# A written TensorE order for the scan stage of a hybrid S5 / attention layer

## The chip, the core and the metric

The kernel runs on one core of one Trainium2 chip. The metric is device time in microseconds: the median of three executions. TensorE (PE, with its weight loads shown apart as PEld), VectorE (DVE), ScalarE (ACT) and GpSimd (POOL) each run their own instruction stream in order; SyncE (SP) issues nearly all the transfers.

## What is computed

One layer of a trunk, on 128 context tokens and 128 latent tokens that share all weights (256 columns in every product), in float32:

```python
mod = silu(cond) @ w_mod + b_mod        # shift1, scale1, gate1, shift2, scale2, gate2
xm  = rmsnorm(x) * (1 + scale1) + shift1
u, q, k, v, gate_ssm, gate_attn = split(xm @ w_in)
S   = s5(u)          # 64 groups x 16 channels, 64 complex states, scanned both ways
S   = (gelu(S) * sigmoid(gelu(S) @ w_glu)) @ w_ssm_o
A   = windowed_attention(q, k, v, sink) @ w_attn_o
x  += gate1 * ((sigmoid(gate_ssm) * S + sigmoid(gate_attn) * A) @ w_out)
x  += gate2 * conv_ffn(rmsnorm(x) * (1 + scale2) + shift2)
```

For each direction of the S5 branch `bu = b_bar @ u`, `h[t] = lam_bar * h[t-1] + bu[t]` and `y += real(c @ h)`; the last states are outputs too.

## The kernel before

Nearly all the work is products with streamed weights. Each weight tile of 512 KB (`[128, 2, 512]` float32) is fetched once into one of five buffers named `raw` (RAW = 5), rounded on ACT to a high part (`hi`, L184), and the remainder is taken on DVE (`lo`, L185); there are three pairs of `hi` and `lo` (HL = 3). Three matmuls then stand for one float32 product (L395, L396, L397). One such tile makes 24 matmuls; it is called an F unit below. The raw buffer is free when `lo` is done.

The modulation `w_mod` is multiplied unsplit: two raw tiles make one burst of matmuls (L263), called M below, and both buffers are held until TensorE has done it. When sixteen such bursts are done, `mod_pp` (L268, L272, L276) moves their sums into place.

`drive()` walks a list of steps. A step is an F unit, half of an M, or a piece of other work. It issues the loads in the list's order as buffers come free, and emits `hi` and `lo` of the next units ahead of the step that uses them, at a raised priority. The list's order is not the order of execution: everything is emitted inside a `TileContext` whose scheduler reorders each engine's instructions by a timeline that it works out itself.

The attention and the S5 branch's set-up are woven into F units of `w_in`. Then comes the scan stage, the subject here. It goes over eight quarters `q` of the state. In each, `bu_mm` multiplies by `BL` (L1375), `rot_in` turns the result (L1388 to L1391), `scans` runs two scans (L1397), `rot_out` turns back into `H` (L1405 to L1407, finals L1409), and `yout` multiplies by `CL` and a small matrix `MI` (L1416, L1425), with a Gelu on ACT (L1428). What the next quarters need is made beside it: `m_gen` makes `MI` (TensorE L1338, ACT L1349 and `dg`, DVE L1344 to L1346); `b_prod` and `b_exp` make `BL`: two products on DVE, an expansion on ACT into `BD` (L1300) and `B` (L1302), and, for each of two directions, two groups of four transposes (L1308) into the only buffer of the PSUM tag `misc`, each copied to `BL` by ACT (L1309); `c_prod` and `c_exp` make `CL` (L1328, L1329); `tables` and `decay` make `tab` and `R`.

Beside the scans TensorE has 56 F units (8 of the attention gate's projection, 16 of `w_attn_o`, 32 of the scan gate's projection with sigmoids on ACT, L672) and 48 bursts M in three groups of sixteen. `weave` deals these evenly into the list of scan steps (`weave(ssm.stages(), (fill, FF0, FF1), (modfill, MF0, MF1))`); the scheduler then decides where each stands. The tail of the attention, which stands ahead of this stage in the list, consists of scores (L625), softmax (DVE L626 to L643, ACT L638), transposes of the weights (L651, copied by L652), products (L658, copied by L663, L664) and four transposes of rows for the convolution (L585).

## Time and profile before

| | |
|---|---|
| median of three executions | 1551.19 us (1549.31 to 1555.21) |
| the profiled execution | 1552.15 us |
| its span, first to last instruction | 1550.1 us |
| TensorE busy | 1491.0 us, 96% |
| weight loads busy | 1311.1 us, 85% |
| VectorE, ScalarE busy | 1007.7 us, 65%; 766.7 us, 49% |
| granted clock of TensorE, mean | 0.99 of 2.4 GHz |
| DMA | 349.18 MB, mean 225 GB/s |

A line of the view by stretches gives a stretch's length, then for each engine (TensorE, its weight loads, VectorE, ScalarE, GpSimd) its busy time and the number of instructions, then the granted clock, the DMA engines' busy share and the rate. A timeline line gives the start, the duration, the engine, the line of the kernel, the operation, the tile written and the tiles read. Matmuls are pipelined, so the distance between starts tells more than the duration of one. Traced matmul counts of L263, L1375 and L1425 are two for each instruction.

### The profile page before, as it was taken

To read this page: it belongs to the slowest core of one execution; us is meant where nothing else is said; L and a number is where in the kernel's file an instruction comes from. 1 tells how busy PE (TensorE), PEld (TensorE's weight loads), DVE (VectorE), ACT (ScalarE), POOL (GpSimd) and SP (SyncE) were. 2 spreads that over 40 slices of the span, in tenths; PEclk is the share of its full clock that TensorE was granted. 3 is DMA by queue.
4 is the path that set the end of the run, shared out by engine and by line. 5 is a ranking of instruction groups with operands and counts; after the bars stand their busy time and mean duration, and the time that the engine had idled before them with its cause. 6 is when DMAs were issued, how large, how long until landed. Compare 5 with 4: busy or idle time off the path is not lost.

```text
span 1550.1 us, 29294 instructions
## 1 busy us (share of the span) xinstructions
PE 1491.0 (96%) x11871; PEld 1311.1 (85%) x11871; DVE 1007.7 (65%) x1541; ACT 766.7 (49%) x1191; POOL 85.7 (6%) x179
## 2 busy tenths in 40 slices
PE   6989999999899999999999999999999999999997
PEld 5758799778677788998689999889999988999986
DVE  4997776468866566765665656655665655666665
ACT  6335537645545666544554544433544543545543
POOL 2000004022321000000000000000000000000000
PEclk9999999999999999999999999999999999999999
DMA  9999754774676677975566676765555565566563
GB/s 352 352 340 321 286 196 157 258 277 156 209 241 238 240 250 274 310 244 192 172 242 235 205 245 201 238 200 190 176 192 181 181 197 191 175 205 197 170 203 123
DMA packets 104246, 349.18 MB, mean 225 GB/s; under 512 B 13900, under 2 KB 16628, under 8 KB 104112
## 3 DMA queue, kind: packets, MB, share of 16 engines
q1 hardware_dynamic: 98576, 344.20, 64.9%
q0 software_dynamic: 5312, 3.05, 0.8%
q8 instruction: 93, 1.52, 0.4%
q14 instruction: 41, 0.34, 0.1%
q10 hardware_dynamic: 224, 0.08, 0.0%
HBM read 343.76 MB, written 2.46 MB: 223 GB/s over the span
## 4 chain that ended last, share of the span: by engine, by line
PE 83%; DMA 8%; DVE 4%; ACT 2%; issue 1%; POOL 1%; SPq 0%; DVEq 0%; ACTq 0%
PE acc L395 16%; PE acc L396 16%; PE acc L397 16%; PE acc L421 8%; PE acc L422 8%; PE acc L423 8%; PE mod L263 5%; DMA raw<-in_w_mod_dram 2%; DMA raw<-in_w_in_dram 2%; PE bu L1375 1%; DVE lo L185 1%; DMA rw<-in_w_mod_dram 1%; DMA U<-u 1%; DMA raw<-in_w_attn_o_dram 1%; ACT hi L184 1%
## 5 line engine op out<-in xcount | busy, mean ns | idle before, releaser
L185 DVE TENSOR_TENSOR lo<-raw,hi 128x1024 fp32r<-128x1024 f32 (+1 forms) x456 | 538.7, 1186 | 444.8 <-ACT hi L184 442.8
L184 ACT ACTIVATE hi<-raw 128x1024 fp32r<-128x1024 f32 (+1 forms) x456 | 468.5, 1029 | 609.1 <-PE acc L397 260.7
L395 PE MATMUL acc<-yh,lo 128*128 128x256 f32 x1408 | 400.0, 284 | 0.0
L396 PE MATMUL acc<-yl,hi 128*128 128x256 f32 x1408 | 398.8, 283 | 0.0
L397 PE MATMUL acc<-yh,hi 128*128 128x256 f32 x1408 | 398.7, 283 | 0.0
L395 PEld LDWEIGHTS acc<-yh,lo 128*128 128x128 f32 x1408 | 270.3, 192 | 8.9 <-DVE lo L185 4.2
L396 PEld LDWEIGHTS acc<-yl,hi 128*128 128x128 f32 x1408 | 270.3, 192 | 0.1
L397 PEld LDWEIGHTS acc<-yh,hi 128*128 128x128 f32 x1408 | 270.2, 192 | 0.0
L395 PE MATMUL acc<-xh,lo 128*128 128x256 f32 x568 | 166.8, 294 | 9.3 <-ACT sig L672 4.8
L396 PE MATMUL acc<-xl,hi 128*128 128x256 f32 x568 | 163.4, 288 | 0.0
L397 PE MATMUL acc<-xh,hi 128*128 128x256 f32 x568 | 163.1, 287 | 0.0
L422 PE MATMUL acc<-lo,ff 128*128 128x512 f32 x352 | 136.8, 389 | 0.0
L423 PE MATMUL acc<-hi,ff 128*128 128x512 f32 x352 | 136.8, 389 | 0.0
L395 PEld LDWEIGHTS acc<-xh,lo 128*128 128x128 f32 x568 | 109.2, 192 | 31.4 <-DVE lo L185 6.9
L421 PE MATMUL acc<-hi,ff 128*128 128x512 f32 x352 | 127.8, 390 | 0.0
L396 PEld LDWEIGHTS acc<-xl,hi 128*128 128x128 f32 x568 | 109.6, 193 | 2.4 <-issue 2.2
L397 PEld LDWEIGHTS acc<-xh,hi 128*128 128x128 f32 x568 | 109.5, 193 | 0.7 <-issue 0.7
L263 PE MATMUL mod<-raw,cst 128*32 128x512 f32 x480 | 72.2, 631 | 8.0 <-DMA raw<-in_w_mod_dram 7.2
L421 PEld LDWEIGHTS acc<-hi,ff 128*128 128x128 f32 x352 | 66.1, 188 | 14.7 <-issue 1.1
L423 PEld LDWEIGHTS acc<-hi,ff 128*128 128x128 f32 x352 | 66.1, 188 | 13.7
L422 PEld LDWEIGHTS acc<-lo,ff 128*128 128x128 f32 x352 | 66.1, 188 | 13.5
L1316 POOL DMA_DIRECT2D U<-u x128 | 62.6, 497 | 159.6 <-PE bu L1375 138.5
(365 smaller groups left out, 2149.3 us busy)
## 6 DMA issues: line engine op xcount, KB each, us to landing
raw<-in_w_up_dram SPq DMA_DIRECT2D x176, 512.0 KB, 4.2
raw<-in_w_mod_dram SPq DMA_DIRECT2D x120, 512.0 KB, 5.1
raw<-in_w_in_dram SPq DMA_DIRECT2D x88, 512.0 KB, 4.5
raw<-in_w_down_dram SPq DMA_DIRECT2D x88, 512.0 KB, 4.3
rw<-in_w_mod_dram SPq DMA_DIRECT2D x56, 512.0 KB, 6.6
raw<-in_w_out_dram SPq DMA_DIRECT2D x32, 512.0 KB, 4.1
rw<-in_w_mod_first_dram SPq DMA_DIRECT2D x16, 512.0 KB, 7.4
raw<-in_w_in_dram SPq DMA_DIRECT2D x32, 256.0 KB, 6.1
```

The costliest lines, as they stand in the source:

```text
L184: ACT(th[:, w], raws[n][:, w], AF.Copy)
L185: TT(tl[:, w], raws[n][:, w], f32(th[:, w]), OP.subtract)
L263: return MM(acc[32 * j:32 * j + 32], cst[:, kt, 6 - 2 * b:38 - 2 * b], rhs, start=start, stop=stop, skip_group_check=True, tile_position=( ...
L395: MM(o, wl, xh, start=start, stop=False, skip_group_check=True)
L396: MM(o, wh, xl, start=False, stop=False, skip_group_check=True)
L397: MM(o, wh, xh, start=False, stop=stop, skip_group_check=True)
L421: MM(accs[s], xl, hi[:, j, :], start=(kt == first), stop=False)
L422: MM(accs[s], xh, lo[:, j, :], start=False, stop=False)
L423: lastmm[0] = MM(accs[s], xh, hi[:, j, :], start=False, stop=(kt == last - 1))
L1316: nc.gpsimd.dma_start(G["U4", qd][32 * e:32 * e + 32, q, :], u[32 * q:32 * q + 32, 64 * e:64 * e + 64])
L1375: MM(bu[:, ri, x], BL[d][:, ri, q, :], u[:, :, ::-1] if d else u, start=(x == 0), stop=True, skip_group_check=True)
```

## The change

Only the scan stage and the pieces that it is made of are changed.

- A region `tc.manual_schedule(engines={PE})` opens ahead of the stage's first step and closes behind its last. Inside it TensorE's instructions run in the order of the program; the other engines are still ordered by the scheduler.
- `weave` is no longer used here. `stages()` now writes one period for each quarter, with the marks `"fill"` (F) and `"mod"` (M) at fixed places: seven F and six M in each. The marks are replaced by the 56 F units and the 48 bursts in their old order.
- A period on TensorE is: `bu_mm`, M, F, M, `m_gen`, F, M, F, transposes, M, transposes, F, F, transposes, M, transposes, F, `yout`, F, M.
- `b_exp` is split: `b_bd` is the expansion on ACT, `b_tr` one group of four transposes with its copy to `BL`. `b_prod` of the next quarter but one stands ahead of `yout`.
- `finals()` stands behind the region.

In the changed file the same code stands some twenty lines lower: `bu_mm` is L1396, the transposes L1329, their copies L1330, the expansion L1318, `MI` L1370, `yout` L1437 and L1446.

```diff
-    weave(ssm.stages(), (fill, FF0, FF1), (modfill, MF0, MF1))
+    plan = ssm.stages()
+    region = ExitStack()
+    step(lambda: region.enter_context(tc.manual_schedule(engines={mybir.EngineType.PE})))
+    left = {"fill": [[u] for u in fill], "mod": []}
...
+    share = {k: (len(v), plan.count(k)) for k, v in left.items()}
...
+    step(region.close)
+    steps.append(ssm.finals())
...
+    def b_tr(qd, d, ri):
+        if (d, ri) == (0, 0):
+            G["BL"] = []
+        if ri == 0:
+            G["BL"].append(S4([128, 2, 4, 128], "BL"))
+        p = PS([128, 4, 128], "misc")
+        for q in range(4):
+            TR(p[:, q, :], G["BD"][:, ri, q].rearrange("p e g c -> p (e g c)"), ident)
+        ACT(G["BL"][d][:, ri], p, AF.Copy)
...
     def stages():
-        st = [s(u_exp, 0), s(u_exp, 1), s(c_exp, 0), s(bu_mm, 0), s(rot_in, 0, 0), s(m_gen, 0), s(rot_in, 0, 1)] + b_side(1) + c_side(1)
+        F, M = "fill", "mod"
+        st = [s(u_exp, 0), s(u_exp, 1), s(c_exp, 0)] + b_side(1)
         for q in range(8):
-            st += [s(scans, q), s(rot_out, q, 0), s(rot_out, q, 1)]
-            if q < 7:
-                st += [s(decay, q + 1), s(bu_mm, q + 1)]
-            if q < 6:
-                st += [s(u_exp, q + 2)]
-            st += [s(yout, q)]
...
-        st.append(Step(finals))
+            n = q + 1
+            more = n < 8
+            st += [s(bu_mm, q), s(rot_in, q, 0), M, s(rot_in, q, 1), F, s(scans, q)]
+            st += [s(decay, n)] if more else []
+            st += [M, s(m_gen, q), F, s(rot_out, q, 0), M]
+            st += [s(b_bd, n, 0)] if more else []
+            st += [s(rot_out, q, 1), F]
+            st += [s(tables, n), s(b_tr, n, 0, 0), M, s(b_tr, n, 0, 1), F] if more else [M, F]
+            st += ([s(b_bd, n, 1)] if more else []) + c_side(n) + [F]
+            st += [s(b_tr, n, 1, 0), M, s(b_tr, n, 1, 1), F] if more else [M, F]
+            st += b_side(n + 1) + [s(yout, q)]
+            st += [s(c_exp, n)] if more else []
+            st += [s(u_exp, q + 2)] if q < 6 else []
+            st += [F, M]
```

Where the instructions stand now is shown at three places; in the rows `x4` is the number of like instructions in a row.

**TensorE at the end of the attention's tail.** `misc<-kc,P` are the transposes of the softmax weights, `misc<-P,..` the products, `misc<-kc,BD` the first transposes of the scan stage, `acc` an F unit and `mod` a burst. Before, around the first row of `bu`:

```order
L396 MATMUL acc<-xl,hi 128x256
L397 MATMUL acc<-xh,hi 128x256
L263 MATMUL mod<-raw,cst 32x512 x4
L1308 MATMUL misc<-kc,BD 128x128 x4
L1375 MATMUL bu<-U_3341,BL 128x64
L395 MATMUL acc<-oh,lo 128x256
L396 MATMUL acc<-ol,hi 128x256
L397 MATMUL acc<-oh,hi 128x256
```

After, up to the first burst:

```order
L658 MATMUL misc<-P,pg 128x512
L651 MATMUL misc<-kc,P 128x128 x8
L658 MATMUL misc<-P,pg 128x512
L658 MATMUL misc<-P,kT 128x512
L1329 MATMUL misc<-kc,BD 128x128 x8
L1396 MATMUL bu<-U_3337,BL 128x64
L585 MATMUL misc<-kc,rows 128x128 x2
L1329 MATMUL misc<-kc,BD 128x128 x8
L1396 MATMUL bu<-U_3337,BL 128x64 x8
L585 MATMUL misc<-kc,rows 128x128
L1396 MATMUL bu<-U_3337,BL 128x64 x7
L263 MATMUL mod<-raw,cst 32x512 x4
```

Before, an M and F units stand between the transposes and behind the first row of `bu`; now the tail's steps and the first `bu` stand in one piece, with the first M behind them.

**ScalarE in the middle of a quarter.** `hi` is the high part of the next F unit, `MI` belongs to `m_gen`, `BL` is the copy out of the transposes' PSUM buffer, `BD` the expansion. Before:

```order
L1309 ACTIVATE BL<-misc 128x512
L1300 ACTIVATE BD<-tB 64x16x16 x2
L184 ACTIVATE hi<-raw 128x1024
L1349 ACTIVATE MI<-y 32x7x32 x4
L1342 ACTIVATE dg<-kc,vecA 128x32
L184 ACTIVATE hi<-raw 128x1024
L1309 ACTIVATE BL<-misc 128x512
L1300 ACTIVATE BD<-tB 64x16x16 x2
```

After:

```order
L184 ACTIVATE hi<-raw 128x1024
L1430 ACTIVATE fin<-H 128x8
L1370 ACTIVATE MI<-y 32x7x32 x4
L1363 ACTIVATE dg<-kc,vecA 128x32
L184 ACTIVATE hi<-raw 128x1024
L1330 ACTIVATE BL<-misc 128x512
L1318 ACTIVATE BD<-tB 64x16x16 x2
L1330 ACTIVATE BL<-misc 128x512
```

Before, the first copy of a direction stands ahead of `MI`, with its own place by the scheduler; now the copy behind the first group of transposes stands behind two `hi`, the four `MI` and `dg`.

**VectorE from one `lo` to the next.** `vv` and `t` behind `bu` are `rot_in`, `vv<-R` the scans, `H` and `t` behind `vv` are `rot_out`, `y` belongs to `m_gen`. Before:

```order
L185 TENSOR_TENSOR lo<-raw,hi 128x1024
L1286 TENSOR_TENSOR tC<-tC,pr 128x384
L1406 TENSOR_TENSOR t_4763<-vv,tab 128x512
L1407 TENSOR_TENSOR H<-H,t_4763 128x16x32
L1406 TENSOR_TENSOR t_4807<-vv,tab 128x512
L1407 TENSOR_TENSOR H<-H,t_4807 128x16x32
L185 TENSOR_TENSOR lo<-raw,hi 128x1024
L1388 TENSOR_TENSOR vv<-bu,tab 128x512
```

After:

```order
L185 TENSOR_TENSOR lo<-raw,hi 128x1024
L1411 TENSOR_TENSOR vv<-vv,t_4897 128x512
L1411 TENSOR_TENSOR vv<-vv,t_4916 128x512
L1412 TENSOR_TENSOR vv<-vv,keep 128x8 x2
L1418 SCALAR_TENSOR_TENSOR vv<-R,vv 128x512 x2
L1426 TENSOR_TENSOR H<-vv,tab 128x16x32
L1365 TENSOR_TENSOR y<-y,dg 128x32
L1427 TENSOR_TENSOR t_5017<-vv,tab 128x512
L1426 TENSOR_TENSOR H<-vv,tab 128x16x32
L1427 TENSOR_TENSOR t_5041<-vv,tab 128x512
L1366 TENSOR_TENSOR y<-y,dg 128x32
L185 TENSOR_TENSOR lo<-raw,hi 128x1024
```

Before, `rot_out` is spread and a `lo` stands on either side of four of its instructions; now the end of `rot_in`, both scans and `rot_out`'s first half stand between two neighbouring `lo`.

## Rows read from the trace of the kernel before

**Rows 1.** Busy time by engine in stages: start:end, length, busy us (instructions), clock, DMA

```profile
260.75:305.00 44.25, 43.34 (x325) 33.92 (x325) 23.74 (x43) 28.24 (x63) 1.80 (x2) 1.00 0.68 250
305.00:608.80 303.80, 280.60 (x3282) 229.25 (x3279) 206.93 (x336) 168.47 (x345) 50.49 (x104) 0.97 0.67 233
608.80:1550.10 941.30, 927.39 (x6410) 853.92 (x6408) 575.13 (x708) 442.14 (x536) 3.05 (x6) 0.99 0.61 204
```

**Rows 2.** The same view: two stretches, and four microseconds behind an idle gap

```profile
305.00:347.00 42.00, 37.83 (x329) 30.73 (x327) 26.11 (x44) 20.16 (x39) 9.31 (x20) 1.00 0.80 282
...
546.00:584.00 38.00, 37.31 (x454) 31.24 (x458) 25.67 (x42) 23.69 (x48) 0.00 (x0) 1.00 0.72 252
...
516.00:520.00 4.00, 4.00 (x19) 2.83 (x20) 2.00 (x2) 2.92 (x4) 0.00 (x0) 0.57 0.08 28
```

**Rows 3.** TensorE's waits, 305 to 608.8: us in total, times, longest

```profile
PE acc L395 <- ACT sig L672: 4.8, 2, 2.9
...
PE misc L1308 <- ACT BL L1309: 1.9, 4, 0.7
```

**Rows 4.** TensorE's timeline: start, us, line, operation, tiles, shapes, count

```profile
456.89 1.04 PE L263 MATMUL mod<-raw,cst 128*32 128x512 f32 x8
457.86 0.39 PE L395 MATMUL acc<-xh,lo 128*128 128x256 f32 x1
...
460.93 1.06 PE L263 MATMUL mod<-raw,cst 128*32 128x512 f32 x8
...
546.20 2.01 PE L1425 MATMUL y<-H,CL 128*32 128x64 f32 x128
...
583.80 2.01 PE L1425 MATMUL y<-H,CL 128*32 128x64 f32 x128
```

**Rows 5.** Costliest groups, 260.75 to 608.8: busy us, mean ns, idle before

```profile
L185 DVE TENSOR_TENSOR lo<-raw,hi 128x1024 fp32r<-128x1024 f32 x59 | 72.0, 1223 | 92.0 <-ACT hi L184 91.9
...
L184 ACT ACTIVATE hi<-raw 128x1024 fp32r<-128x1024 f32 x58 | 61.2, 1057 | 107.4 <-DMA raw<-in_w_in_dram 61.1 <-DMA raw<-in_w_attn_o_dram 25.0 <-DVE vv L1391 6.5
...
L1397 DVE TENSOR_TENSOR_SCAN vv<-R,vv 128x512 f32<-128x512 f32 x16 | 19.3, 1214 | 0.0
...
L1309 ACT ACTIVATE BL<-misc 128x512 f32<-128x512 f32 x32 | 19.0, 593 | 12.0 <-PE misc L1308 11.7
...
L1349 ACT ACTIVATE MI<-y 32x224 f32<-32x224 f32 x32 | 11.1, 347 | 3.4 <-DVE y L1346 2.9
...
L1388 DVE TENSOR_TENSOR vv<-bu,tab 128x512 f32<-128x512 f32 x16 | 11.0, 686 | 8.3 <-PE bu L1375 8.3
```

**Rows 6.** Chain of waits that ended last, 400 to 420: start, us, what

```profile
401.27 1.06 ACT hi L184
402.36 0.61 ACT BL L1309
403.01 0.66 PE misc L1308 x4
...
407.81 3.57 DMA raw<-in_w_in_dram
...
413.74 4.79 DMA raw<-in_w_in_dram
```

**Rows 7.** ScalarE's timeline in the attention tail

```profile
278.47 1.28 ACT L638 ACT_TABLE_LOAD   x1 [1.85 <-DVE st L633]
...
282.61 0.42 ACT L1300 ACTIVATE BD<-tB 64x256 f32<-64x256 f32 x1
...
286.59 1.25 ACT L1328 ACTIVATE CL<-bct 64x128 f32<-64x128 f32 x4
```

**Rows 8.** TensorE's groups from 260.75 to 325.9, the attention's tail

```profile
L396 PE MATMUL acc<-xl,hi 128*128 128x256 f32 x72 | 21.3, 296 | 0.0
...
L263 PE MATMUL mod<-raw,cst 128*32 128x512 f32 x79 | 11.4, 604 | 2.2 <-DMA raw<-in_w_mod_dram 2.2
...
L396 PE MATMUL acc<-ol,hi 128*128 128x256 f32 x26 | 7.3, 282 | 0.0
```

More of the change, by code (lines that the diff above doesn't have):

```diff
@@ L729, in tile_hybrid_step @@
         modfill += mod_steps(list(range(i, i + 4)))
-    weave(ssm.stages(), (fill, FF0, FF1), (modfill, MF0, MF1))
+    plan = ssm.stages()
+    region = ExitStack()
+    step(lambda: region.enter_context(tc.manual_schedule(engines={mybir.EngineType.PE})))
+    left = {"fill": [[u] for u in fill], "mod": []}
+    while modfill:
+        end = burst(modfill, 0)
+        left["mod"].append(modfill[:end])
+        modfill = modfill[end:]
+    share = {k: (len(v), plan.count(k)) for k, v in left.items()}
+    seen = dict.fromkeys(left, 0)
+    for x in plan:
+        if x in left:
+            seen[x] += 1
+            n, m = share[x]
+            for _ in range(n * seen[x] // m - n * (seen[x] - 1) // m):
+                steps.extend(left[x].pop(0))
+        else:
+            steps.append(x)
+    step(region.close)
+    steps.append(ssm.finals())
     for i in range(NGS, 4):
@@ L1302, in b_exp @@
                     ACT(G["B0"][hs, ri, :, h, :], tB[hs, ri, 0], AF.Copy)
-        BL = S4([128, 2, 4, 128], "BL")
-        G["BL"].append(BL)
-        for ri in range(2):
-            p = PS([128, 4, 128], "misc")
-            for q in range(4):
-                TR(p[:, q, :], BD[:, ri, q].rearrange("p e g c -> p (e g c)"), ident)
-            ACT(BL[:, ri], p, AF.Copy)
+    def b_tr(qd, d, ri):
[7 more added lines that the diff above has]
+        ACT(G["BL"][d][:, ri], p, AF.Copy)
     def u_exp(qd):
```

17 lines of the change are left out of this document (6 added, 11 removed).

## The prediction

> **What bounds the kernel now.** I read the stretches first, then TensorE's waits inside the scan stage, then the timeline at the places that the new order touches. TensorE is the bound throughout: it is busy 927.39 of 941.30 us behind the stage, which the change leaves alone, and 43.34 of 44.25 in the attention's tail; only in the scan stage does it stand visibly, 280.60 of 303.80 us at a mean clock of 0.97 [rows 1]. So the change has at most some 23 us of idle time to win there, plus what the lower clock costs. The named waits are long but few: twice the sigmoid's eviction, 4.8 us together, the longer 2.9 [rows 3], and after the 2.9 the next four microseconds ran at 0.57 of full speed, of the two levels mostly the lower [rows 2]. The copies of transposes cost only 1.9 us in all [rows 3].
>
> What a quarter needs is read from the best one. From `yout` at 546.20 to `yout` at 583.80 are 37.60 us with seven F and six M, as in one period of the new order [rows 4]; the stretch around it holds 38.00 - 37.31 = 0.69 us of idle time [rows 2]. A period without gaps is so 36.9 us. It splits into M, 457.86 - 456.89 = 0.97; F, 460.93 - 457.86 = 3.07 [rows 4]; 7 x 3.07 + 6 x 0.97 = 27.3; the other 9.6 are `bu`, `yout`, `m_gen` and the transposes.
>
> **The attention's tail.** The order shows a thing that the diff doesn't: because TensorE is in program order from the stage's first step, F and M can't be drawn forward any more into the tail ahead of it. Before, from 260.75 to 325.9 TensorE did 72 + 26 triples of F matmuls, eight to a unit, so 12.2 F, and 79/8 = 9.9 bursts M beside the tail [rows 8]. After, one F is left there; 11.2 x 3.07 + 9.9 x 0.97 = 44 us of cover are gone from the tail and stand behind it. They have to be done in any case, so the price is only what the bare tail waits for itself. Its own matmuls take 65.1 - 37.5 (F) - 9.6 (M) - 1.1 (the `m_gen` there, an estimate from its 32 matmuls) - 2.9 (idle) = 14 us; with the one F, 17. No wait between them would put the first M at 278. But each group needs the last one's result: scores, a table load and eight exponentials (4.1 us from 278.47 to 282.61), expansions and `CL` to 287.8 [rows 7], a PSUM copy of about 0.6 behind each group of transposes [rows 5], reductions on VectorE. On ScalarE alone that is another table load of 1.28 [rows 7] with a full-tile copy like `hi`, 1.06 [rows 5], the 4.1, six copies 3.5, the expansions and `CL` 4.3, four `BL` copies 2.4, together 17; reductions, scaling and `ol` on VectorE 5 more, an estimate by durations like 0.69 [rows 5] for seven such steps. Nothing of the two overlaps if every step waits: 260.75 + 14 + 3 + 17 + 5 = 299.75, less about 4 where ScalarE's expansions run beside the second head's products. I take 295.5, close to the serial end, as the chain has no second strand; the ends are 278 and 300. TensorE stands some 17 us in that time, in pieces; one of them lasts over the 4.1 us of the exponentials, so the clock falls once as in rows 2, which I put at 3 us (0 to 5).
>
> **The period, its stalls.** With written places, TensorE waits wherever an input is late; before, the scheduler put other work there. I went through the dependencies of one period with the durations of before and find two late ones.
>
> The third F. Its `lo` stands on VectorE behind both halves of `rot_in`, another `lo`, both scans and the first half of `rot_out`: ten such steps at 0.61 from start to start (0.69 alone, they overlap by 0.08), two scans 2.3, two `lo` 2.4, small ones 0.5, in all 11.3 us from the end of `bu` [rows 5]. TensorE gets there after three M, two F and `m_gen`, 9.9 us. It stands 1.4 us.
>
> The second group of transposes. It needs the PSUM buffer `misc` free, so the copy of the first group. ScalarE has this copy in seven of seven quarters behind the `hi` of the fourth F, `fin`, four `MI`, `dg` and the `hi` of the fifth F. Those two F get the buffers that the third M frees, so their loads start at its end: 3.57 [rows 6], two `hi` 2.1, `MI` 1.4, `fin` and `dg` 0.5, the copy 0.6 [rows 5], hand-overs 0.2: 8.35 us. TensorE is there after 1.4 + 3.07 + 0.4 + 0.97 = 5.7 (stall, F, transposes, M). It stands 2.65 us. That ScalarE holds a copy behind a `hi` whose load is late is seen once in before's chain: `hi` at 401.27, copy at 402.36, transposes at 403.01 [rows 6]. The Trainium skill, page "Perfetto Trace Analysis", section "Matmuls", asks that independent groups rotate through PSUM banks so that one's eviction overlaps the next, and here both groups go through one. By that rule a second bank takes the 2.65 out. The trace disagrees so far, with 1.9 us for the copies in the whole stage [rows 3]; by this row the stall would be near nothing, and the sum 18.6 us lower.
>
> The row comes from an order that the scheduler could fit to the copies, the new one can't give way; so I take the worked-out 2.65. Together 4.05 us a period, seven times (the last has no transposes, but I leave the rest as is): 28. The lower end is 0.7 a period, as in the best quarter; the upper, with loads of 4.79 instead of 3.57 [rows 6], 4.05 + 2 x 1.2 = 6.5.
>
> Without stalls I found: `m_gen`'s chain (it has the time of an F and more behind `yout`), the second pair of transposes, whose copies have no `hi` with a late load ahead, the sixth and seventh F, `H` for `yout`. `fin`, `tables`, `decay` are hidden by VectorE being 68% and ScalarE 55% busy in the stage [rows 1]; if that cover went, each would cost about its own 0.6. The sigmoids keep their table loads, but the F units that follow now have other work between; I put 2 us in all for these and for `mod_pp` (the sigmoids cost 4.8 before [rows 3]). `finals` and the split of `b_exp` add no instruction and stand beside other work: nothing, at most 1.
>
> **The sum.** First M 295.5; eight periods of 36.9 less about 5 (the first `bu` is in the tail, the last period has no transposes, half of the 9.6): 290; stalls 28; clock behind the tail 3; sigmoids 2. The stage would end at 618.5 to 619 where it ended at 608.8, so +10. The profiled execution took 1552.15 us, 2.05 more than its span and 0.96 more than the median; 1552.15 + 10 - 1 = 1561 against the median.
>
> **Rivals.** First, the other side: the written order flows. If the copy gets past the late `hi`, by loads earlier than I have them, and VectorE's queue drains in time, each period is like the best quarter of before, 0.7 us of idle. Then the stage ends at 295.5 + 290 + 5 + 5 = 595.5, -13, and the time is about 1538. It decides from a stall of 4.05 - 10/7 = 2.6 us a period: below that the kernel is faster. For it: the three large gaps of before, with the slow clock behind them, are gone, and the idle 23 us with them. Against: the two queues shown by the order. The Trainium skill, "Perfetto Trace Analysis", section "Optimization Strategy", advises to interleave regimes whose bound differs. By it the even mixing in the quarters gives this time; by the same rule the bare tail loses. No row of before separates the two.
>
> Second, the repeated stalls pull the clock down. After one wait of 2.9 us four microseconds went at 0.57 [rows 2], which loses 1.7. If the 2.65 does the same each period, 7 x 2 = 14 more: about 1575. For it, the likeness of the two gaps; against, the stretch from 305 to 347, where TensorE lacks 42.00 - 37.83 = 4.2 us in several gaps, and the clock is 1.00 [rows 2].
>
> Third, loads slower than 3.57: with five buffers and 19 tiles of 512 KB in 41 us the rate is 243 GB/s, about the 252 of the best quarter [rows 2], but issued in pairs. At 4.79 the two stalls grow to 6.5, 7 x 2.4 = 17 more: 1578.
>
> That the change doesn't do what it says I leave out, as the order shows TensorE in the written sequence.
>
> **How the numbers follow.** My forecast, 1553 to 1570, has 0.45; the first rival 0.23; the second 0.2; the third 0.12. For a range that leaves out no more than 2 in 10, I go from 1538, the first rival's middle, to 1583, past the middles of the second and third. Half a per cent, 7.8 us, is about what a measurement of this kernel can tell from no change: faster means under 1543, slower over 1559. Of the first rival four fifths lie under 1543; of the forecast, four tenths lie under 1559, mostly by an earlier end of the tail (each microsecond there counts once) or a smaller stall (each tenth counts seven times). So faster 0.19, same 0.22, slower 0.59.
>
> **What would show it.** Right: first M at 293 to 298; in each period TensorE waits for `BL` once, 2 to 3 us, ahead of the second group of transposes, and once about 1.4 for `lo` ahead of the third F; periods of 40 to 42 us from `yout` to `yout`; behind the stage the same length as before, 941 us. Wrong: `BL` waits of under 1 us, or periods under 39 us (then the loads came earlier or ScalarE's copies were not held up); first M before 285; a clock under 0.95 over the periods (second rival); load times over 4.5 (third).

## The result, and the profile after

| | before | after |
|---|---|---|
| median | 1552.33 us (1549.31 to 1555.21) | 1590.16 us (1585.42 to 1595.18) |
| ratio to before, 95% interval | | 1.0244 (1.0206 to 1.0282) |
| the profiled execution, its span | 1552.15, 1550.1 us | 1585.42, 1583.4 us |
| TensorE busy | 1491.0 us | 1498.3 us |
| granted clock of TensorE, mean | 0.990 | 0.977 |

Slower, as forecast, but by 38 us and not by 10: the time lies outside the range of 1538 to 1583. Each median here is of four executions; in the table of the kernel before it was of three.

A few executions were far slower than the others of their kernel (4256.13 us in one run below, 2268.59 in another) and are left out of all times and ratios. The others of one kernel lie up to 13 us apart, and each trace is of one execution, so a difference of a few microseconds between two traces is a hint and no proof.

The first view is that of [rows 1], for the kernel after: the attention's tail up to the first burst M (303.6), the rest of the scan stage up to the first matmul that reads its result (640.9), and the rest of the kernel. Columns as there: length, busy time (instructions) of TensorE, weight loads, VectorE, ScalarE and GpSimd, clock, DMA share, GB/s.

```profile
260.75:303.64 42.89, 27.59 (x123) 19.33 (x125) 22.45 (x49) 27.54 (x69) 3.27 (x6) 0.67 0.12 39
303.64:640.90 337.26, 302.58 (x3475) 252.42 (x3475) 203.14 (x329) 172.57 (x341) 50.05 (x102) 0.96 0.69 236
640.90:1583.40 942.50, 928.12 (x6417) 853.91 (x6417) 576.28 (x709) 439.82 (x533) 2.07 (x4) 0.99 0.62 205
...
336.12:633.79 297.67, 266.69 (x3069) 223.35 (x3068) 176.93 (x285) 152.34 (x303) 42.20 (x86) 0.97 0.69 237
```

And the same view of before, with the stage in one piece (the first such matmul was at 608.6):

```profile
260.75:608.62 347.87, 323.76 (x3603) 263.01 (x3603) 230.49 (x379) 196.53 (x407) 52.28 (x106) 0.98 0.67 235
608.62:1550.10 941.48, 927.58 (x6413) 854.08 (x6410) 575.31 (x708) 442.32 (x536) 3.05 (x6) 0.99 0.61 204
```

All of the loss is in the stage: 42.89 + 337.26 = 380.15 us against 347.87, 32.3 more; behind it 942.50 against 941.48. TensorE is idle 50.0 us of the stage (before 24.1), and busy 330.17 (before 323.76) with the same matmuls. Of the 32.3, then, 25.9 are idle time and 6.4 the same work taking longer. (Busy time is not the clock alone: the fastest run below counts 323.56 us for these matmuls at a clock of 1.00.) The last row of the first fence is seven periods, `yout` to `yout`: 42.5 us each, 38.1 busy, 4.4 idle.

TensorE's waits in these seven periods (total, times, longest), to be held against [rows 3]:

```profile
PE acc L395 <- DVE lo L185: 15.4, 9, 3.2
PE misc L1329 <- ACT BL L1330: 11.5, 5, 3.2
PE mod L272 <- DVE macc L268: 2.4, 1, 2.4
PE mod L272 <- DVE vv L1412: 1.7, 1, 1.7
```

These four are all of the 297.67 - 266.69 = 31.0 us. The copies of the transposes, 1.9 us in the whole stage before, are now 11.5 in seven periods and 14.1 in the stage; the `lo` of an F unit stands first; the sigmoids are gone. Two other rows of this view show the tail: the stretch in which the softmax's weights are made, and one with transposes and `bu`.

```profile
275.00:280.00 5.00, 0.72 (x1) 0.00 (x0) 3.64 (x12) 4.96 (x24) 0.00 (x0) 0.50 0.01 2
295.00:300.00 5.00, 4.31 (x22) 3.91 (x20) 4.74 (x9) 3.25 (x6) 0.30 (x1) 0.50 0.07 18
```

At 275 TensorE stands while ScalarE works; twenty microseconds on, it works 4.31 of 5 us at the lower level of its clock, 0.50 of full speed. In [rows 1] this part of the kernel ran at 1.00, with 43.34 of 44.25 us busy.

### The profile page after: what moved, and what is told of

Read it like the earlier page. It is cut to its first block, busy times and chain, and to the rows that moved or that the text cites. A ratio compares the mean times of both kernels' runs of the same rounds, so it can differ in the third digit from the quotient of the medians.

```text
span 1583.4 us, 29296 instructions
## 1 busy us (share of the span) xinstructions
PE 1498.3 (95%) x11871; PEld 1320.7 (83%) x11871; DVE 1003.3 (63%) x1541; ACT 767.0 (48%) x1190; POOL 85.7 (5%) x179
## 3 DMA queue, kind: packets, MB, share of 16 engines
q8 instruction: 93, 1.52, 0.4%
## 4 chain that ended last, share of the span: by engine, by line
PE 74%; DMA 4%; ACT 2%; DVE 1%; issue 1%; DVEq 0%; SPq 0%; ACTq 0%
PE acc L395 15%; PE acc L396 15%; PE acc L397 15%; PE acc L421 7%; PE acc L423 7%; PE acc L422 7%; PE mod L263 3%; DMA raw<-in_w_in_dram 3%; PE bu L1396 2%; PE misc L1329 1%; ACT hi L184 1%; PE y L1446 1%; DMA raw<-in_w_attn_o_dram 1%; PE y L1437 1%; DMA raw<-in_w_mod_dram 1%
## 5 line engine op out<-in xcount | busy, mean ns | idle before, releaser
L422 PEld LDWEIGHTS acc<-lo,ff 128*128 128x128 f32 x352 | 66.1, 188 | 13.5
L922 ACT ACTIVATE ab<-acc,cw 128x256 f32<-128x256 f32 x88 | 46.9, 558 | 44.0 <-DVE ab L924 34.8
```

Source lines behind the costliest of these rows:

```text
L422: MM(accs[s], xh, lo[:, j, :], start=False, stop=False)
L922: ACT(y, x, AF.Identity, scale=cw[:, 1, col:col + 1], bias=cw[:, 3, col:col + 1])
```

## The experiments

Three questions: is it the list of steps or TensorE's fixed order; what the bare tail costs; and what makes the two stalls in each period. The edits are to the kernel after. Ratios are to executions of the kernel before that were taken beside each run (their medians lie between 1550.9 and 1555.5 us), so runs are compared by their ratios and intervals.

### The same list, left to the scheduler

```diff
-    step(lambda: region.enter_context(tc.manual_schedule(engines={mybir.EngineType.PE})))
```

> The new list of steps with everything split and moved as in the change, but no region: the scheduler orders TensorE as it did before. Theory A (the fixed order is what costs): tail covered and stalls filled as before, time 1545 to 1562. Rival C (the list is what costs, through later m_gen, c_prod, b_prod or the single place of each F and M): 1572 to 1592 without the region too.

Measured: 1555.46 us, 1.0017 (0.9998 to 1.0035). Its stage, to the first matmul on the result:

```profile
260.75:608.22 347.47, 323.61 (x3621) 265.89 (x3620) 228.23 (x384) 200.15 (x413) 52.31 (x106) 0.99 0.68 234
```

The list alone changes nothing: 347.47 us against 347.87, with the same idle time and the same busy time. The 35 us between 1555.46 and 1590.16 are the price of the region: inside it TensorE is held to the list's order, and none of its work can be drawn ahead of it.

### Work for the tail

Eight more F (one group of the gate's projection) and eight M are woven into the attention ahead of the region, 8 x 3.07 + 8 x 0.97 = 32 us of work by [rows 4].

```diff
-NGA2, NGS, SF0, ATT1 = 3, 4, 0.6, 1.0
+NGA2, NGS, SF0, ATT1 = 4, 4, 0.6, 1.0
...
-    weave(late, (att, 0.0, ATT1), (ssm.first(), SF0, 1.0))
+    modfill = []
+    for i in range(8, 20, 4):
+        modfill += mod_steps(list(range(i, i + 4)))
+    weave(late, (att, 0.0, ATT1), (ssm.first(), SF0, 1.0), (modfill[:16], 0.6, 1.0))
+    modfill = modfill[16:]
...
```

> Eight F units (the attention gate's last group) and eight bursts M are taken out of the written region and woven into the attention's tail ahead of it, where the scheduler places them; each period keeps its order, with six F and five M on average. Theory A (the bare tail is a price of its own): TensorE lost some 26 us between 260 and 303.6, 15 of them idle, the rest at the low clock; with cover there the first M of the region comes at most 3 us after the last step of the tail, the clock stays at 1.00 in the tail, and the time falls by 20 to 26 us, to 1564 to 1570. Rival B (the stage is bound by its loads and five buffers, so work done early only waits later): the tail is filled but the periods don't get shorter by the work taken out (3.07 + 0.97 = 4 us each), and the time falls by under 8 us, to 1582 or more.

Measured: 1572.97 us, 1.0139 (1.0104 to 1.0175), between the two expectations. The stretches are the tail and the first period behind it:

```profile
260.75:306.21 45.46, 43.61 (x307) 31.71 (x306) 23.17 (x42) 27.18 (x60) 0.95 (x1) 1.00 0.67 232
306.21:351.83 45.62, 39.10 (x291) 31.53 (x289) 32.78 (x58) 24.92 (x50) 11.05 (x22) 0.85 0.64 216
```

The tail is again full, 43.61 of 45.46 us at a clock of 1.00, as in [rows 1]. But of the 32 us moved, the stage ends only 15.7 earlier (625.23 instead of 640.90). The rest is lost behind it. TensorE stands 6.5 us in the first period, where the clock is 0.85, and with eight M gone ahead a group of sixteen ends at another place: at 380.75 `mod_pp` had kept TensorE waiting for 8.63 us, for a step (`macc`) in VectorE's queue.

To mend that, six M went ahead instead of eight:

```diff
-    weave(late, (att, 0.0, ATT1), (ssm.first(), SF0, 1.0), (modfill[:16], 0.6, 1.0))
-    modfill = modfill[16:]
+    weave(late, (att, 0.0, ATT1), (ssm.first(), SF0, 1.0), (modfill[:12], 0.6, 1.0))
+    modfill = modfill[12:]
```

> As the run with the filled tail, with six bursts M instead of eight taken into the tail, so that each group of sixteen ends at the last M of a period and mod_pp stands ahead of bu. The wait of 8.6 us for macc, which VectorE's queue held up in the middle of a quarter, should go: time 6 to 10 us below that run's 1574.9, at 1565 to 1569. If instead it was part of the same shortage that the BL waits show, the BL waits (16.8 us) grow by as much, and the time stays within 3 us of 1575.

Measured: 1585.15 us, 1.0190 (1.0139 to 1.0242). The wait of `mod_pp` is nearly gone, 1.7 us in all, but in the seven periods behind the first (349.11 to 630.05) F units now wait 20.9 us for `lo`. In the kernel with eight M ahead, that wait was 4.0 us in the whole stage. Why two bursts more or less should switch it on and off I did not settle; the expectation was wrong. As times, the two versions are not clearly apart: their intervals overlap, and so do those of six M and of the kernel after.

### Which queue makes the two stalls

Both stalls are where the prediction put them, ahead of the third F and of the second transposes. First I moved the late operations. TensorE's order is the list's; ScalarE's and VectorE's are worked out anew by the scheduler for each version. The second transposes behind the fourth F:

```diff
-            st += [s(tables, n), s(b_tr, n, 0, 0), M, s(b_tr, n, 0, 1), F] if more else [M, F]
+            st += [s(tables, n), s(b_tr, n, 0, 0), M, F, s(b_tr, n, 0, 1)] if more else [M, F]
```

> One change in the period: the second group of transposes stands behind the fourth F instead of ahead of it, so the copy of the first group has 3.07 us more. Theory A (the copy to BL on ScalarE stands behind two hi): the BL waits, 14.1 us in six periods, fall under 3, the clock's fall behind them goes with them in part, and the time falls by 12 to 20 us, to 1570 to 1578. Rival B (bound by loads): the same time turns up as a wait for lo ahead of the fourth or fifth F, the sum of waits stays near 33 us, and the time stays within 5 us of 1590.

Measured: 1585.33 us, 1.0218 (1.0181 to 1.0255); the waits of its seven periods:

```profile
PE acc L395 <- DVE lo L185: 21.8, 12, 3.8
PE misc L1329 <- ACT BL L1330: 5.2, 6, 2.2
```

The time is not told apart from that of the kernel after. The transposes' wait falls by 6.3 us, from 11.5 to 5.2, and `lo`'s rises by 6.4, from 15.4 to 21.8. Most of the rise is at F units behind the third: the fourth, now first in line, stands 3.6 us in four of the periods for its own `lo`. The third F stands 2.3 us longer, over the seven periods, than in the kernel after.

In the next, the fourth M stands ahead of the third F as well:

```diff
-            st += [s(rot_out, q, 1), F]
-            st += [s(tables, n), s(b_tr, n, 0, 0), M, F, s(b_tr, n, 0, 1)] if more else [M, F]
+            st += [s(rot_out, q, 1), M, F]
+            st += [s(tables, n), s(b_tr, n, 0, 0), F, s(b_tr, n, 0, 1)] if more else [F]
```

> As the run with the late transposes, and the fourth M stands ahead of the third F, so that TensorE comes to that F 0.97 us later. Theory A (lo of the third F stands on VectorE behind rot_in, the scans and rot_out): the wait ahead of the third F, 0.9 to 3.3 us in each period, falls by 1 us each, 7 us or a little more with the clock; the time is 6 to 10 us below the run with the late transposes alone, 1560 to 1571. Rival B: the fourth M now waits for its own loads by the same amount, and the time equals that of the run with the late transposes within 3 us.

Measured: 1588.39 us, 1.0238 (1.0211 to 1.0266):

```profile
PE acc L395 <- DVE lo L185: 17.3, 7, 4.2
PE mod L263 <- DMA raw<-in_w_mod_dram: 5.0, 6, 1.4
```

The M itself now waits for its tiles, as the second expectation had it, so late loads are part of the matter. The first expectation was not put to a clean test: in all seven periods VectorE now does more of `rot_out` (L1428) ahead of this `lo`. These seven periods have less idle time, 28.1 us, in longer pieces, and at a clock of 0.94 the same matmuls take 271.64 us:

```profile
335.22:634.91 299.69, 271.64 (x3069) 229.75 (x3068) 176.95 (x285) 151.84 (x304) 42.19 (x86) 0.94 0.69 237
```

One period of the kernel after shows both, loads and queues: SyncE's loads, then ScalarE (with what ended the idle time before each), VectorE and TensorE, start and duration in us.

```profile
350.99 0.33 SPq L155 DMA_DIRECT2D raw<-in_w_attn_o_dram  x1
...
355.77 0.80 SPq L155 DMA_DIRECT2D raw<-in_w_attn_o_dram  x2
```

```profile
355.09 1.06 ACT L184 ACTIVATE hi<-raw 128x1024 fp32r<-128x1024 f32 x1 [2.24 <-DMA raw<-in_w_attn_o_dram]
...
361.04 1.06 ACT L184 ACTIVATE hi<-raw 128x1024 fp32r<-128x1024 f32 x1 [2.55 <-DMA raw<-in_w_attn_o_dram]
...
362.11 1.41 ACT L1370 ACTIVATE MI<-y 32x224 f32<-32x224 f32 x4
...
363.77 1.04 ACT L184 ACTIVATE hi<-raw 128x1024 fp32r<-128x1024 f32 x1
364.84 0.60 ACT L1330 ACTIVATE BL<-misc 128x512 f32<-128x512 f32 x1
```

```profile
349.04 1.22 DVE L185 TENSOR_TENSOR lo<-raw,hi 128x1024 fp32r<-128x1024 f32 x1 [0.61 <-ACT hi L184]
...
351.59 2.34 DVE L1418 TENSOR_TENSOR_SCAN vv<-R,vv 128x512 f32<-128x512 f32 x2
...
356.43 1.21 DVE L185 TENSOR_TENSOR lo<-raw,hi 128x1024 fp32r<-128x1024 f32 x1
```

```profile
357.70 0.39 PE L395 MATMUL acc<-oh,lo 128*128 128x256 f32 x1 [1.96 <-DVE lo L185]
...
361.20 1.06 PE L263 MATMUL mod<-raw,cst 128*32 128x512 f32 x8
365.49 0.66 PE L1329 MATMUL misc<-kc,BD 128*128 128x128 f32 x4 [3.22 <-ACT BL L1330]
```

The third F: its tile is asked for at 350.99, when the second M frees a buffer, and `hi` starts at 355.09 after 2.24 us in which ScalarE had nothing but the load to wait for. `lo` follows at 356.43, F at 357.70. But `hi` had ended at 356.15, and VectorE was not idle for a moment from the `lo` of the second F (349.04) to this one: the end of `rot_in`, the scans and half of `rot_out` stand between, as the prediction counted them. So it is in all seven periods: `hi` ends 0.05 to 1.52 us before its `lo` begins, and VectorE is busy up to it. What ends last is VectorE's queue, with the load close behind it. The load that TensorE's wait does show is that of the second F: VectorE stands for it ahead of that F's `lo` (0.61 us here, 0 to 1.92 in the seven periods, 0.88 on average) and everything behind moves by as much.

The fourth and fifth F: asked for at 355.77, at the end of the third M; `hi` at 361.04, 5.3 us later, then `MI`, the next `hi` and only then the copy at 364.84, for which the transposes stand 3.22 us. Here ScalarE waited for the load first (2.55 us).

So I turned F and M around: the third F ahead of the third M, the fourth M behind the second transposes. F needs one buffer, and gives it back at `lo`; M needs two, until TensorE is done.

```diff
-            st += [M, s(m_gen, q), F, s(rot_out, q, 0), M]
+            st += [M, s(m_gen, q), F, s(rot_out, q, 0), F]
...
-            st += [s(rot_out, q, 1), F]
-            st += [s(tables, n), s(b_tr, n, 0, 0), M, s(b_tr, n, 0, 1), F] if more else [M, F]
-            st += ([s(b_bd, n, 1)] if more else []) + c_side(n) + [F]
+            st += [s(rot_out, q, 1), M]
+            st += [s(tables, n), s(b_tr, n, 0, 0), F, s(b_tr, n, 0, 1)] if more else [F]
+            st += ([s(b_bd, n, 1)] if more else []) + c_side(n) + [M, F]
```

> Another written order with the same number of F and M in a period: the third F stands ahead of the third M, and the fourth M behind the second group of transposes (bu, M, F, M, m_gen, F, F, M, transposes, F, transposes, M, F, transposes, M, transposes, F, yout, F, M). A burst M holds two of the five raw buffers from its load to its execution; in this order the third F's load is issued ahead of the third M's. Theory B (late loads: a buffer comes free only when TensorE has done an earlier M): the waits for lo and for BL, 29.5 us from 303 to 636, fall under 15, with part of the clock's falls, and the time is 15 to 25 us below 1590, at 1565 to 1575. Theory A (VectorE's and ScalarE's queues hold the third F's lo and the copy): the third F is now reached 0.97 us earlier and waits the longer, its waits grow from 15 to 20 us or more; the time stays at 1583 or above.

Measured: 1581.88 us, 1.0184 (1.0145 to 1.0223), which overlaps a little with the interval of the kernel after. It falls between the two expectations: `lo` and `BL` waits are 20.4 us, not under 15, and have not grown either. Seven periods, and their waits:

```profile
336.28:625.06 288.78, 261.03 (x3070) 216.58 (x3069) 176.64 (x286) 152.85 (x304) 42.36 (x86) 0.99 0.71 246
```

```profile
PE misc L1329 <- ACT BL L1330: 10.5, 6, 2.2
PE acc L395 <- DVE lo L185: 9.9, 8, 1.7
```

297.67 us become 288.78. Only 3.2 of these 8.9 are idle time; 5.7 are busy time, for as many matmuls, at a clock of 0.99 instead of 0.97. Waits at F and transposes are shorter here (2.2 at most, not 3.2) and the clock is higher, but the length of a wait does not decide it. In the kernel after, the 40 us with the waits of 1.96 and 3.22 shown above ran at 1.00, and six microseconds behind the wait of 3.25 that ended at 444.87 at 0.72:

```profile
340.00:380.00 40.00, 34.82 (x421) 28.85 (x423) 25.95 (x44) 22.32 (x44) 7.81 (x16) 1.00 0.75 253
445.00:451.00 6.00, 5.95 (x36) 4.87 (x36) 5.00 (x11) 3.39 (x9) 0.00 (x0) 0.72 0.42 143
```

The test of the buffers is a sixth `raw` buffer. The room for it comes from the small tables, cut to a part of themselves and used again for the rest; the instructions are as many and the outputs differ:

```diff
-RAW, HL, W4, NS4, W2, LOADS = 5, 3, 18, 5, 3, 5
+RAW, HL, W4, NS4, W2, LOADS = 6, 3, 18, 5, 3, 5
...
-    cst = cpool.tile([128, 16, 38], F32, name="cst")
+    cst = cpool.tile([128, 4, 38], F32, name="cst")
...
-    cw = cpool.tile([128, 4, 88], F32, name="cw")
+    cw = cpool.tile([128, 4, 4], F32, name="cw")
...
```

> The changed kernel with a sixth raw buffer. To make room for it the convolution's weights are kept as 4 of 88 columns and the modulation's input as 4 of 16, each used again for the others; the same instructions run and the outputs differ. Theory B (late loads): lo and BL waits from 303 to 636 fall from 29.5 us to under 12, and the time by 15 to 25 us, to 1565 to 1575; the rest of the kernel gains at most 3 us. Theory A (queues of VectorE and ScalarE): the waits stay within 6 us of 29.5, and the time within 6 us of 1590.

Measured: 1578.42 us, 1.0147 (1.0112 to 1.0182):

```profile
336.04:625.79 289.75, 266.32 (x3070) 222.83 (x3069) 176.15 (x286) 153.40 (x304) 42.39 (x86) 0.96 0.70 242
```

```profile
PE acc L395 <- DVE lo L185: 7.0, 5, 3.3
...
PE misc L1329 <- ACT BL L1330: 6.5, 5, 2.9
```

The two named waits fall by half, 26.9 to 13.5 us, and this run's interval lies below that of the kernel after: nearly what the expectation gave to late loads. But the sixth buffer did not only bring loads earlier. The scheduler sorted the other engines anew: in all seven periods the third F's `lo` now stands ahead of three of `rot_out`'s steps, 6.6 to 7.2 us behind the start of `rot_in` where it was 9.8 to 11.8, and ScalarE makes the copy to `BL` ahead of `MI`. The row is this run's third `lo`, in the period whose `rot_in` began at 348.27:

```profile
354.90 1.22 DVE L185 TENSOR_TENSOR lo<-raw,hi 128x1024 fp32r<-128x1024 f32 x1
```

So this run does not part the buffers from the queues. SyncE's waits, here of the kernel after and then of this one (336 to 626), only change their name: less for an M to free a buffer, more for a `lo`, 173.5 us together and then 160.6.

```profile
SPq L155 <- PE mod L263: 120.2, 40, 5.8
SPq L155 <- DVE lo L185: 53.3, 31, 3.0
```

```profile
SPq L155 <- DVE lo L185: 87.7, 39, 4.2
SPq L155 <- PE mod L263: 72.9, 27, 5.0
```

Nor is SyncE's wait for an M a loss by itself: it was 101.5 us in the kernel before (305 to 600), 114.8 in the order with F ahead (336 to 626), and 128.4 in the fastest version below (305 to 590).

The idle time of the seven periods falls only from 31.0 to 23.4 us, since `mod_pp` waits longer (7.0 us, before 4.1) and a sigmoid waits again (2.8). The Trainium skill, page "Perfetto Trace Analysis", section "Optimization Strategy", says of a gap that repeats for a stretch of the kernel on the engine that should be saturated that it can mean too few buffers. This run agrees that a buffer more takes half of these gaps away, together with the new order on the other engines. The rule of the Trainium skill, same page, section "Matmuls", which the prediction weighed and set aside, a second PSUM bank for the transposes, speaks of the BL stall; a second buffer for `misc` was not tried.

The other answer to the BL stall is another engine for the copy:

```diff
-        ACT(G["BL"][d][:, ri], p, AF.Copy)
+        CP(G["BL"][d][:, ri], p) if (d, ri) == (0, 0) else ACT(G["BL"][d][:, ri], p, AF.Copy)
```

> The copy behind the first group of transposes is made by VectorE instead of ScalarE, where it stands behind the lo of the fifth F instead of behind its hi. Theory A for this wait (the copy stands behind work on late loads, on whichever engine): the wait ahead of the second group moves to VectorE and grows by about a lo, 1.2 us each; 5 to 12 us slower, 1595 to 1602. Rival (ScalarE's own load of MI, dg and expansions is what delays it): the wait falls by half, time 1578 to 1585.

Measured: 1591.26 us, 1.0236 (1.0208 to 1.0264), the same as after and between the two expectations. The waits of its seven periods:

```profile
PE misc L1329 <- DVE BL L1330: 11.0, 4, 3.1
```

VectorE's queue also holds the copy, which the expectation put behind the `lo` of a late load. The wait has moved to that queue and has not grown. That the late load is the cause in either queue is the likeliest reading; it was not shown apart.

Both helps together, the tail with six M and the order with F ahead:

> The filled tail with six M and the other written order together. If tail and period are two prices that add: 1590 - 22 - 20 = 1548, 1540 to 1556, about the kernel before. If loads bound the stage as a whole, the two don't add, and the time is that of the better one alone, 1563 or more.

Measured: 1577.21 us, 1.0148 (1.0119 to 1.0177). The first expectation had taken tail and order to be worth some 20 us each, which neither gave. The time is in the range of the second (1563 or more), but not for its reason: what the two gave alone does add up, within the interval: 1.0244 less 0.0054 (six M) and 0.0060 (the order) is 1.0130. The tail with eight M and the order was not run; the eight M alone gave 1.0139.

### What the clock costs

Twelve matmuls without use (128 columns, into a spare PSUM buffer) at each of the two places where TensorE stands, so that it is hardly idle there:

```diff
+    def keep_busy(n):
+        p = PS([128, 128], "bu")
+        for _ in range(n):
+            MM(p, ident, ident, start=True, stop=True)
...
-            st += [s(rot_out, q, 1), F]
-            st += [s(tables, n), s(b_tr, n, 0, 0), M, s(b_tr, n, 0, 1), F] if more else [M, F]
+            st += [s(rot_out, q, 1), s(keep_busy, 12), F]
+            st += [s(tables, n), s(b_tr, n, 0, 0), M, s(keep_busy, 12), s(b_tr, n, 0, 1), F] if more else [M, F]
```

> The changed kernel with extra work: at each of the two places where TensorE waits in a period, twelve 128-column matmuls whose result nobody reads stand in front of the waiting instruction (1.4 us at full speed, in a bank that is free there). They change no input's arrival. Theory C (a wait of some 2 us and more lets the granted clock fall for the following microseconds, and this, not the wait itself, is what the prediction missed): the clock over the eight quarters rises from 0.96 to 0.99, the other matmuls take some 8 us less, and the kernel gets 5 to 10 us faster although it does more, at 1580 to 1585. Rival D (the low clock has another cause, such as the whole load of the chip or the mixture of fp32 and fp32r matmuls): the clock stays at 0.96 and the time at 1590 or up to 5 us above.

Measured: 1596.62 us, 1.0276 (1.0251 to 1.0302). One such place on TensorE's timeline, and the seven periods:

```profile
359.09 2.94 PE L1473 MATMUL bu<-kc 128*128 128x128 f32 x24
361.79 0.36 PE L395 MATMUL acc<-oh,lo 128*128 128x256 f32 x1
...
411.90 4.58 PE L1473 MATMUL bu<-kc 128*128 128x128 f32 x24
```

```profile
339.54:642.20 302.66, 294.59 (x3381) 251.70 (x3380) 177.86 (x285) 151.13 (x303) 42.22 (x86) 0.99 0.67 232
```

The filler takes 361.79 - 359.09 = 2.70 us a place (0.225 a matmul, shown as two), twice what I had planned, at twelve of thirteen places, and 4.42 at one, behind a wait of `mod_pp`: 36.8 us. What is left, 294.59 - 36.8 = 257.8 us, is the kernel's own work, which took 266.69 in the kernel after. So the lower clock cost about 8.9 us in these seven periods, and at 0.99 a period's work is 257.8 / 7 = 36.8 us, the prediction's 36.9. But filler and remaining idle time are 44.9 us where 31.0 were idle, so nothing is won; the expected 1580 to 1585 failed by that.

With five instead of twelve at each place the filler fits the gaps:

```diff
-            st += [s(rot_out, q, 1), s(keep_busy, 12), F]
+            st += [s(rot_out, q, 1), s(keep_busy, 5), F]
```

> As the run with extra matmuls at the two waiting places, with five instead of twelve at each. One of them measured 0.225 us, so twelve took 2.7 us, more than the waits of 2.1 and 2.4 that they stood in; five take 1.1 us, inside the waits. Theory C (the granted clock falls behind a wait of 2 us and more, and costs the following matmuls): waits of at most 1 to 2 us remain at the two places, the clock over the eight quarters is 0.98 or more instead of 0.96, TensorE's other matmuls take 5 to 10 us less, and the kernel is 3 to 9 us faster than the changed one, 1581 to 1587. Rival D (other cause): time 1589 to 1596.

Measured: 1591.52 us, 1.0261 (1.0243 to 1.0279). The clock rises to 0.98 as expected, but the filler takes about 15 us, the work still about 266, and the time does not fall. What the clock costs was not had back by either filler.

The same in the tail, 24 matmuls behind the products of each group of heads:

```diff
+        p = PS([128, 128], "y")
+        for _ in range(24):
+            MM(p, ident, f32(oh)[:, 0:128], start=True, stop=True)
```

> The changed kernel with 24 matmuls of 128 columns behind the product of each head in the attention's tail, on the head's own output, whose result nobody reads; the scheduler puts them into the gaps of the bare tail. Theory C: the granted clock from 265 to 303, 0.50 to 0.74 now, stays at 0.9 or above, the tail's own steps take half as long as now, and the first M comes at 294 to 299 instead of 303.6; the kernel is 4 to 10 us faster, at 1580 to 1586. Rival D: the clock stays low, the extra matmuls delay the tail, and the time is 1592 or more.

Measured: 1601.87 us, 1.0301 (1.0271 to 1.0331). The first stretch shown for after, another in the tail, and two behind it:

```profile
275.00:280.00 5.00, 5.00 (x46) 5.00 (x45) 4.40 (x11) 3.25 (x13) 0.95 (x1) 1.00 0.10 36
...
285.00:290.00 5.00, 4.31 (x23) 4.13 (x23) 0.69 (x1) 1.83 (x5) 0.00 (x0) 0.66 0.00 0
...
305.00:310.00 5.00, 2.88 (x12) 2.16 (x13) 3.52 (x9) 2.04 (x5) 1.48 (x4) 0.67 0.09 18
310.00:315.00 5.00, 5.00 (x26) 5.00 (x26) 2.71 (x6) 4.33 (x9) 0.00 (x0) 0.50 0.00 0
```

The clock is 1.00 in the stretches up to 305 but for 285 to 290, at the price of some 5.5 us a group on the chain. It falls between 305 and 310, where TensorE is busy 2.88 of the 5 us, and is at 0.50 in the next five although TensorE is busy all of them.

With eight matmuls a group:

```diff
+        for _ in range(8):
```

> As the run with extra matmuls in the tail, with 8 instead of 24 behind each head (1.8 us at full speed, since one took 0.225 us). Theory C: they fit into the tail's gaps, the clock stays above 0.8 on average from 265 to 303 instead of 0.6, the first M of the region comes at 297 to 302 instead of 303.6, and the kernel is 2 to 7 us faster than the changed one, 1583 to 1588. Rival D, or gaps that lie elsewhere than the extra work: 1590 to 1598.

Measured: 1597.12 us, 1.0294 (1.0277 to 1.0311); the tail's clock rises from 0.67 to 0.81 and the first M comes at 306.57, 3 us later. The tail's clock is thus shown in its rows, but its share of the time was not isolated: every filler lengthened the chain.

### The order with F ahead, left to the scheduler

The order with F ahead of M, without the region: the list sets the order of loads and leaves TensorE to the scheduler.

```diff
-    step(lambda: region.enter_context(tc.manual_schedule(engines={mybir.EngineType.PE})))
...
-            st += [M, s(m_gen, q), F, s(rot_out, q, 0), M]
+            st += [M, s(m_gen, q), F, s(rot_out, q, 0), F]
```

(and the other lines of the F-ahead order, as above)

> The second written order's list (third F ahead of third M) without the region, so that it sets only the order of loads and the scheduler places TensorE's work. If the list without a region is neutral, as the change's own list was (1555.5 against 1553.4): 1548 to 1560. If the order of loads that served the written order better (1582 against 1590) also serves the free one: 1540 to 1549, under the kernel before.

Measured: 1546.59 us, 0.9945 (0.9925 to 0.9965): half a per cent faster than the kernel before, small, but clear of the scatter (1543.70 to 1549.90, against 1551.76 to 1562.63 for the kernel before beside it).

```profile
260.75:597.64 336.89, 323.56 (x3597) 261.85 (x3596) 225.05 (x378) 196.80 (x408) 50.20 (x102) 1.00 0.70 242
```

```profile
PE acc L395 <- DVE lo L185: 4.2, 4, 1.4
PE mod L263 <- DMA raw<-in_w_mod_dram: 2.4, 4, 0.9
```

The stage takes 336.89 us (before 347.87) with 13.3 idle (before 24.1), and no wait of these two kinds is over 1.4 us. With the list of the change and no region, the waits for M's tiles alone had been 11.0 us (seven, the longest 2.9). So the idea of mixing F and M by hand has a gain in it, as a list that the scheduler may depart from. I take it to act as an order of loads; the list also sets the order in which the scheduler is given the work, and the two were not parted.

## Why the prediction was wrong in size

**The step that failed** is the clock, and so the time that the work takes. The stage was to end at 618.5 to 619 and ended at 640.9, 22 us later. Idle time was forecast well: 17 + 28 + 2 = 47 us, measured 50.0. Busy time was not: 17 + 290 of work and 3 for the clock, 310 us, measured 27.59 + 302.58 = 330.2. The prediction had put the work at durations of full speed, the clock at one fall of 3 us, and left the clock behind the repeated stalls out of the sum, as a rival. Of the 20 us of busy time, 8.9 are shown as clock by the filled stalls; in the tail the rows at 0.50 say the same, without a run that isolates it; the rest was not separated. A check was at hand: [rows 1] has 43.34 + 280.60 = 323.9 us of busy time for the same matmuls before, 17 more than 307.

**The tail.** The mechanism was right: without F and M beside it, the tail waits for its own chain. Idle time 15.3 us (predicted 17). First M predicted at 295.5, with 3 us for the clock 298.5; measured 303.56. The term that failed is "the clock falls once", 3 us with an upper end of 5. The clock's mean over the whole tail is 0.67 (1.00 up to 270, 0.50 from 275 to 285), and the work put at 17 us took 27.59. A filled tail gave 15.7 us back at the stage's end, about half of the 32 us of work that went into it.

**The period.** Its work, 36.9 us, holds: 36.8 when the clock is at 0.99. The two stalls stand at the places named, ahead of the third F (predicted 1.4 us, measured 0.88 to 3.25, mean 2.1) and of the second transposes (predicted 2.65, mean 2.4; once `mod_pp` stands there instead). Together 4.5 against 4.05, and all idle time behind the first M 34.7 against the 30 of stalls and sigmoids.

For the third F the cause held. From `bu` to the end of its `lo` VectorE took 11.0 to 13.0 us, 12.1 on average (predicted 11.3), and TensorE came after 9.8 (predicted 9.9). What was put at nothing is VectorE's wait for the load of the second F, 0.88 us on average. For the transposes the chain held link by link (load, two `hi`, `MI`, `dg`, copy), and its load took 5.3 us, not 3.57. That the stall came out near the forecast is in part luck: in the period shown the chain took 9.70 us and not 8.35, but TensorE also came later, after 6.53 and not 5.7 (the prediction's own terms give 5.84, and so a stall of 2.5).

What holds both stalls up is not parted. Loads that wait for buffers and queues on VectorE and ScalarE end within 1.5 us of each other at the third F. Moving one operation mostly moved the wait (the late transposes, the early fourth M, the copy on VectorE); a sixth buffer halved both waits, with the other engines' order changed as well.

**The rivals.** The first, that the order flows, fell: each period has its two stalls. The second, that the repeated stalls pull the clock down, came true in part, and my reason against it failed. I took 305 to 347 of before, several short gaps at a clock of 1.00, as like the new order. A stretch like it is there, 340 to 380, at 1.00; but over the seven periods the clock is 0.97. It was priced at 14 us and cost 8.9. My mark for it, a clock under 0.95, was too coarse: 0.97 over 297.67 us is already this loss. The third, slower loads, rested on one row: 3.57 us is a quick load. The median of all 512 KB loads in the stage was 5.0 us before and is 5.1 now, so its mark, over 4.5 us, told nothing. For F's own tiles it came true: 4.0 and 4.4 before (`w_in`, `w_attn_o`), 5.4 and 5.5 now. The price was nearer 5 us of idle time than 17. I gave these two 0.32 as cases that exclude each other; they came together, and on top of them the tail's clock.

**The sum.** Of the 22 us, about 5 are in the tail and 17 behind it. Of the 17, idle time is 4.7 and busy time 12.6 (302.58 against 290): 8.4 in the seven periods (266.69 against 7 x 36.9), which the filled stalls show to be clock, and some 4 in the first period, where the clock is 0.91, and around the last, which were not separated. Behind the stage 942.5 us, as predicted (941). The other 7 of the miss of 29: 1.0 behind the stage, and the profiled execution of after lies 4.7 us under its median where that of before lay 0.96 over.

What stays open: the tail's clock in microseconds, whether loads or queues weigh more in the two stalls, why `lo` waits with six M ahead and not with eight, and a second PSUM buffer for the transposes.

## What to carry to other kernels

A written order for an engine is only as good as the worst arrival on each of its inputs. Where a scheduler had placed work into such waits, writing the order costs them all (1.0017 with the list alone, 1.0244 with the list as TensorE's order); put the knowledge into the list that it works from instead (0.9945). A fixed region also cuts off the work that used to flow out of it into the stretch ahead, so look at what that stretch had beside it. And if a stall moves rather than goes when one operation is moved, look at all its inputs: here the load, its buffer and the engine's queue came due within 1.5 us of each other. When a buffer is added, look whether the scheduler has sorted the other engines anew before the gain is put down to the buffer.

## What the runs showed of the hardware

- After gaps, the work itself can be slow: TensorE at 0.50 of full speed at 295 to 300 us while busy 4.31 of 5 us, and at 310 to 315 in the filled tail while busy all 5, behind five microseconds with 2.88 busy. Price a gap with the work behind it, not alone.
- The same matmuls of seven periods took 266.69 us in the kernel after (clock 0.97), 271.64 with the fourth M ahead (0.94), 266.32 with a sixth buffer (0.96), 263.21 with the late transposes (0.98), 261.03 in the F-ahead order (0.99) and about 257.8 with the gaps filled (0.99). The longest single wait does not sort them: 3.2, 4.2, 4.1, 3.8, 2.9 and 2.3 us.
- A 512 KB load took 5.0 us in the stage before and 5.1 after (medians; 3.3 to 8.7 and 3.4 to 7.0), at 235 GB/s on average (after, 336 to 626). One of 3.57 [rows 6] is near the low end.
- A float32 matmul of 128 by 128 with 128 columns, back to back, took 0.225 us; two of them are recorded for each.
